# Two v projections called from the attention loop, and bias masks added in pairs, in a two-block transformer kernel

## The chip, the cores and the metric

The kernel runs on one core of a Trainium2 chip, as one program. The metric is the device time of that program in microseconds, the median over several runs. The core's engines work side by side, each through its own queue of instructions in order: TensorE (PE) multiplies matrices into PSUM, VectorE (DVE), ScalarE (ACT) and GpSimd (POOL) do the element-wise work, SyncE (SP) issues the loads.

## The reference

256 tokens of width 1024 go through two blocks. The first (MoBA attention, gated delta rule, a hierarchical mixture of experts) is not touched. The second block is this, cut to what matters:

```python
h = _modulate(_rms_norm(x, norm1_g), shift, scale)
q_a, k_a, v_a, q_b, k_b, v_b = _in_proj(h, w_in)            # latents
_, k_ac, v_ac, _, k_bc, v_bc = _in_proj(h_ctx, w_in)        # context
# heads a: rms norm of q and k per head, axial rope, window attention, sink
# heads b: rms norm of q and k per head, neighbourhood attention with bias rpb
o = concat([rms_norm(o_a) , rms_norm(o_b)]) * on            # per type, over its 512 columns
x = x + gate1 * (o @ w_out)
h = _modulate(_rms_norm(x, norm2_g), shift2, scale2)
x = x + gate2 * ((silu(h @ w_gate) * (h @ w_up)) @ w_down)
```

Both kinds of heads attend to 256 latent tokens and 256 context tokens, with 8 heads of 64 columns each.

## The kernel before, in words

**Products.** A product in block 2 is exact to nearly fp32: each operand is split into a high and a low part in fp32r, and `mm3` (L196) issues three matmuls, high by high, high by low, low by high (they are booked at L99). `split_w` (L168) splits a block of 256 weight rows or columns: ACT copies the high part in two pieces (L185), DVE or POOL subtracts for the low part in four (L192).

**Projections.** `proj_lat` (L1518) projects the latents on 256 columns of w_in: 48 matmuls into one PSUM bank of tag "big". The list `jobs` sets their order: k and v of heads a, k of heads b, then by `LORD = "bav"` q of heads b, q of heads a (`qa`, two halves), v of heads b (columns 1792 and 2048, tile `lvbp`, two halves). What is done with each product (`use`) comes one job later (`LAG`): for q `qk_heads` (head norm, rope at L1120 to L1123, transposes `pqk`, high and low halves at L1167 and L1171), for v a copy by DVE (L1539). With each projection the weights of the next are split, pieces 1 and 3 of the low part on POOL.

**Bias.** The bias of heads b comes by DMA into `bias0` and `bias1` (four heads each). `bias_mask` (L1571) adds a column mask to one head's bias on POOL; `BMU` says behind which unit.

**Attention.** The attention is cut in 16 units: type (a, then b), pair of heads m, half of the queries qt. `scores` (L1579) multiplies q by k into two "big" banks, adds the window mask or the bias by another matmul, takes the maximum on DVE (L1597), the exponential on ACT (L1607), and scales by the reciprocal sum, one head on ACT (L1616), the other on DVE (L1618). `turn` (L1623) transposes the probabilities through the two "tr" banks (`ptp`), one copy out by ACT, one by DVE (L1629). `outputs` multiplies by v into a bank `po` that two units share. `finish` (L1645) squares `po` on ACT (L1647), sums the squares over the columns with matmuls by a column of ones (`psq`, bank "sm"), copies the sum to `ssab` on DVE (L1651), and writes the scaled output as high and low part to `moh` and `mol` (L1652, L1653). The loop over the units computes the scores one unit ahead, and calls `hooks(i)` behind unit i.

**After.** `out_part` multiplies `moh`, `mol` by the four row blocks of w_out (wq0 to wq3; `pqa`, `pqb` in "big"), then the feed-forward part follows in 11 blocks (fg, fu, fd).

**What sets the order.** The framework's scheduler orders each engine's instructions when the program is built; the source order, the buffers and the few `after` calls bound it. PSUM in this stage: four "big" banks, two "tr", one "sm", one "mo". In SBUF a ring of nine 1 MB slots (`NRING`) holds the raw weight blocks, qa, qb, kAb0 and the biases; a slot is given again when its readers are done.

Of the kernel before, what the change touches and what calls it, by code (L numbers as in the profile page):

```python
# [10 lines left out]
F32R = mybir.dt.float32r  # L11
BF16 = mybir.dt.bfloat16
AF = mybir.ActivationFunctionType
ALU = mybir.AluOpType
# [3 lines left out]
P = 128  # L18
# [87 lines left out]
def tile_kernel(ctx: ExitStack, tc: tile.TileContext, I, out, dbg=None):  # L106
    nc = tc.nc
    PE, ACT, DVE, POOL, SP = Ordered(tc, nc.tensor), nc.scalar, nc.vector, nc.gpsimd, nc.sync
# [5 lines left out]
    S_ = {}  # L114
# [14 lines left out]
    def at(shape, tag, name, bufs=1, dt=F32):  # L129
        return S_["act"].tile(shape, dt, tag=tag, name=name, bufs=bufs)  # L130

    def open_part(name, psum):

        st = ExitStack()
        S_["tmp"] = st.enter_context(tc.tile_pool(name="tmp_" + name, bufs=1, reuse_waits="tile"))
        S_["ps"] = st.enter_context(tc.tile_pool(name="ps_" + name, bufs=1, space=PSUM, reuse_waits="tile"))
        S_["banks"] = psum
        return st
# [4 lines left out]
    def tmp_(shape, tag, name, bufs=1, dt=F32):  # L143
        return S_["tmp"].tile(shape, dt, tag=tag, name=name, bufs=bufs)

    def pt_(shape, tag, name):
        return S_["ps"].tile(shape, F32, tag=tag, name=name, bufs=S_["banks"][tag])

    def psm(shape, name, tag="sm"):
        return pso.tile(shape, F32, tag=tag, name=name)  # L150
# [174 lines left out]
    hth = at([P, 8, 256], "hth", "hth", dt=F32R)  # L325
    htl = at([P, 8, 256], "htl", "htl", dt=F32R)
# [393 lines left out]
    for tt in range(2):  # L720
        p = pt_([P, 4, P], "rec", "po")
# [149 lines left out]
    part = open_part("c1", {"gu": 2, "y": 2})  # L871
# [7 lines left out]
    for tt in range(2):  # L879
        ts = slice(tt * P, (tt + 1) * P)  # L880
        for i in range(2):
            p = pt_([P, 4, P], ("gu", "y")[tt], "pt")
# [6 lines left out]
    for tt in range(2):  # L889
        jk = tmp_([P, D], "jk", "jk", bufs=2, dt=BF16)  # L890
        if tt == 0:
            i = jk_ins = ACT.activation(jk, x[:, 0], AF.Square, accum_out=ssq[:, 0:1])
        else:
            i = DVE.scalar_tensor_tensor(jk, x[:, 1], 1.0, x[:, 1], op0=ALU.mult, op1=ALU.mult, accum_out=ssq[:, 1:2])
        if JKA[tt]:
            after(i, copies[2 + tt])
    v = tmp_([P, 2], "rv", "r1v")
# [149 lines left out]
    kvw = {}  # L1047
# [9 lines left out]
    part = open_part("c2", {"gu": 1, "y": 2, "tr": 1})  # L1057
# [45 lines left out]
    def head_norm(p, nh, dst, name):  # L1103

        src = p.rearrange("p t (n d) -> p t n d", d=64)
        sq = tmp_([P, 2, nh, 64], "hsq", "hsq", bufs=2)
        S_["hsq"] = ACT.activation(sq, src, AF.Square)
        ss = tmp_([P, 2, nh], "hss", "hss", bufs=4)
        DVE.tensor_reduce(ss, sq, axis=AX.X, op=ALU.add)
        r = rstd_of(ss.rearrange("p a b -> p (a b)"), 2 * nh, 1.0 / 64, EPS, name).rearrange("p (a b) -> p a b", a=2)  # L1110
        DVE.tensor_tensor(dst, src, bc(r, 64), op=ALU.mult)

    def do_rope(src, nh, i, dst):

        t2 = tmp_([P, 2, nh, 64], "hsq", "rt2", bufs=2)
        cosg, sing = rgt[:, i, :, 0], rgt[:, i, :, 1]
        for h in range(2):
            for b in range(2):
                o, i_ = 32 * h + 16 * b, 32 * h + 16 * (1 - b)
                DVE.tensor_tensor(t2[:, :, :, o:o + 16], src[:, :, :, i_:i_ + 16],  # L1120
                                  sing[:, :, None, o:o + 16].to_broadcast([P, 2, nh, 16]), op=ALU.mult)
        DVE.tensor_tensor(dst, src, cosg[:, :, None, :].to_broadcast([P, 2, nh, 64]), op=ALU.mult)
        DVE.tensor_tensor(dst, dst, t2, op=ALU.add)  # L1123

    def kv_a(p, s, tag):

        DVE.tensor_copy(va[s], p[:, :, P:256])
        kn_ = tmp_([P, 2, 2, 64], "qn_", "kn_", bufs=2)
        head_norm(p[:, :, 0:P], 2, kn_, "rka")
        if s == 0:  # L1130
            kr = tmp_([P, 2, 2, 64], "qn_", "kr", bufs=2)
            do_rope(kn_, 2, 1, kr)
            kn_ = kr
        kd = tmp_([P, 2, 2, 2, 64], "hsq", "kd", bufs=2)
        for tt in range(2):
            DVE.tensor_copy(kd[:, tt], kn_[:, tt][:, :, None, :].to_broadcast([P, 2, 2, 64]))
        pt = pt_([P, 2, 256], tag, "pka")
        for kvh in range(2):
            for tt in range(2):
                PE.transpose(pt[:, kvh, tt * P:(tt + 1) * P], kd[:, tt, kvh].rearrange("p a b -> p (a b)"), ident)  # L1140
        if s == 0:
            ACT.activation(kAa[s], pt, AF.Copy)
            DVE.tensor_tensor(kLa[s], pt, kAa[s], op=ALU.subtract)
        else:
            ACT.activation(kAa[s], pt, AF.Copy, scale=gcol[:, 1:2])
            DVE.scalar_tensor_tensor(kLa[s], pt, gcol[:, 1:2], kAa[s], op0=ALU.mult, op1=ALU.subtract)
# [32 lines left out]
    kAa, kLa, kAb, kLb, va, vb = ([None] * 2 for _ in range(6))  # L1179
# [96 lines left out]
    for u in range(8):  # L1276
        if u == IFU:
# [6 lines left out]
            part = open_part("ov", {"gu": 2, "y": 2})  # L1284
            overflow()
            part.close()
            part = open_part("c3", {"gu": 1, "y": 1, "tr": 1, "cx": 1})
# [28 lines left out]
        for i, (w, nm) in enumerate(((wg_, "eg"), (wu_, "eu"), (wd_, "ed"))):  # L1316
            if len(first[u]) == i:
                first[u].append([wexp(w, u, q, nm) for q in range(4)])
            if u >= IFU and i < 2 and CTX[u][i]:
                c0 = CTX[u][i][0]  # L1320
# [37 lines left out]
        p = pt_([P, 256], "tr", "pst")  # L1358
# [98 lines left out]
    for c0 in [c for part in LORD for c in {"v": (1792,), "a": (0, 256), "b": (768, 1024)}[part]]:  # L1457
        kvw[c0] = load_block(cols(w_in2, c0), "lat")
    hth, htl = mod_T(xf, [ss[:, 4, i:i + 1] for i in range(2)], mod[:, 1], mod[:, 0], "l",
                     lambda: kv_tiles(0, lambda shape, nm, dt: vb0 if nm == "vb0" else at(shape, nm, nm, dt=dt)))  # L1460
# [51 lines left out]
    qa = ring_tile("qa").rearrange("p (i m c) -> p i m c", i=2, m=4)  # L1512

    latw = {512: lka_w, 1280: lkb_w}
    seq = [1280, 1536] + [c for part in LORD for c in {"v": (1792, 2048), "a": (0, 256), "b": (768, 1024)}[part]]
    NEXT = dict(zip(seq, seq[1:]))

    def proj_lat(c0, name):  # L1518
        hi, lo = latw[c0]
        if c0 in NEXT:  # L1520
            n = NEXT[c0]
            latw[n] = split_w(kvw[n], "lat", pool=PLAT)
        p = pt_([P, 2, 256], "big", name + "p")
        for tt in range(2):
            ts = slice(tt * P, (tt + 1) * P)
            for k in range(8):
                mm3(p[:, tt], hth[:, k, ts], htl[:, k, ts], hi[:, k], lo[:, k], k == 0, k == 7)
        return p
# [3 lines left out]
    def uses(part):  # L1532

        for half in range(2):
            if part == "k":
                yield 1280 + 256 * half, "lkb", lambda p, half=half: qk_heads(p, half, 3, "tr", s=0)
            elif part == "v":
                vs = vb[0][:, :, half * 256:half * 256 + 256]
                yield 1792 + 256 * half, "lvb", lambda p, vs=vs: DVE.tensor_copy(vs, p)  # L1539
            elif part == "a":  # L1540
                yield 256 * half, "lq", lambda p, half=half: qk_heads(p, half, 0, "tr", q=qa)
            else:
                yield 768 + 256 * half, "lq", lambda p, half=half: qk_heads(p, half, 2, "tr", q=qb)

    ready = at([P, 1], "ready", "ready")
    jobs = [(512, "lka", lambda p: kv_a(p, 0, "tr"))] + [j for part in "k" + LORD for j in uses(part)]
    lag = []
    for n, (c0, name, use) in enumerate(jobs):
        if n == 3:
            after(ACT.activation(ready, mhalf[:, :1], AF.Exp), S_["hi"])  # L1550
        p = proj_lat(c0, name)
# [5 lines left out]
    bias = []  # L1557
# [9 lines left out]

    cm = cst3[:, C_CM:C_CM + 64]

    def bias_mask(h):  # L1570
        return POOL.tensor_tensor(bias[h], bias[h], cm[:, None, :].to_broadcast([P, 6, 64]), op=ALU.add)  # L1571


    moh = at([P, 8, 256], "hth", "moh", dt=F32R)
    mol = at([P, 8, 256], "htl", "mol", dt=F32R)
    rab = []
    ssab = at([P, 2, 2, 4], "ssab", "ssab")

# [65 lines left out]
    def finish(typ, m, po_):  # L1644
        k = 4 * typ + m  # L1645
        osq = at([P, 256], "mt", "osq2", bufs=3)
        ACT.activation(osq, po_, AF.Square)  # L1647
        psq = psm([P, 2], "psq")
        for tt in range(2):
            PE.matmul(psq[:, tt:tt + 1], lhsT=osq[:, tt * P:(tt + 1) * P], rhs=ones1, start=True, stop=True)  # L1650
        DVE.tensor_copy(ssab[:, typ, :, m], psq)  # L1651
        ACT.activation(moh[:, k], po_, AF.Copy, scale=onT[:, k:k + 1])  # L1652
        DVE.scalar_tensor_tensor(mol[:, k], po_, onT[:, k:k + 1], moh[:, k], op0=ALU.mult, op1=ALU.subtract)  # L1653
        if m == 3:
            ssum = at([P, 2], "ssum", "ssum", bufs=2)
            DVE.tensor_reduce(ssum, ssab[:, typ], axis=AX.X, op=ALU.add)
            rab.append(rstd_of(ssum, 2, 1.0 / 512, EPS, f"rab{typ}"))
# [11 lines left out]
    def hooks(i):  # L1669

        nonlocal g1B
        if i in G1U:
            g1B = row_bc(mod[:, 2, :, 0], kvc.tile([P, D], F32, tag="fB", name="g1B"))
        for h in BMU.get(i, ()):
            bias_mask(h)
        if i in WQU:
            w_blk2[WQU.index(i)] = w_block(WQU.index(i))
            after(S_["hi0"], S_["exp"])
# [59 lines left out]
    hth, htl = mod_T(x, norm_rows(x, "rf"), mod[:, 4], mod[:, 3], "f")  # L1738
# [70 lines left out]
PLAT = (1, 3)  # L1809
# [22 lines left out]
LORD = "bav"  # L1832
AORD = False
LATE = True
G1U = (5,)
BMU = {4: (0, 1), 5: (2, 3, 4, 5, 6, 7)}
WQU = (8, 10)
MORD = True
FOUT = [4, 2, 2, 2]
# [38 lines left out]
```

## Time and profile before

| what | us |
|---|---|
| runs, median (lowest, highest) | 837.55 (834.93, 837.75) |
| the profiled execution's own time | 832.61 |
| its span, first to last instruction | 830.8 |
| mean granted TensorE clock in it | 0.972 |
| PE busy (x instructions) | 752.4 (x6276) |
| DVE busy | 425.1 (x933) |
| ACT busy | 301.7 (x533) |
| POOL busy | 108.1 (x94) |

Times in the trace count from the start of the span. The projections of v run from 509.6 to 522 us, the attention units from 525.7 to about 617, the out-projection ends at about 620, the feed-forward part fills the rest. A bracket behind a row of the timeline tells how long the engine was idle before it, and who ended that.

### The profile page before, as it was taken

Reading aid. Unit: us, or ns where it says so; the run is one execution under the profiler, and the core shown is the slowest. Engines: PE = TensorE matmul, PEld = TensorE weight load, DVE = VectorE, ACT = ScalarE, POOL = GpSimd, SP = SyncE. Lnnn points to the kernel's source line nnn. Section 1 sums busy time; section 2 is a strip of 40 time slices with the busy share of each in tenths; the row PEclk is TensorE's granted clock in tenths of the full one; section 3 lists DMA queues with packets and bytes.
Section 4 is the critical chain, followed back from the end, with each engine's and each line's share of the span. In section 5 each row is a group of like instructions: output and inputs, shape, how many; then the busy total and the mean of one; then the engine's idle time right before and its main releaser. Section 6 shows DMA issues by size and latency. Waiting matters only on the chain.

```text
span 830.8 us, 15017 instructions
## 1 busy us (share of the span) xinstructions
PE 752.4 (91%) x6276; PEld 604.0 (73%) x6276; DVE 425.1 (51%) x933; ACT 301.7 (36%) x533; POOL 108.1 (13%) x94
## 2 busy tenths in 40 slices
PE   7999999999799976787778999699987999999997
PEld 7887887966644424374544889688866999999996
DVE  5767543465712212203222789988655654545545
ACT  5532233443420010001114663488515343443441
POOL 5011000053000000000000476400122100000000
PEclk9999999999799998999999999999998999999999
DMA  7999778577589999999989416011441754555201
GB/s 214 356 386 388 283 284 302 203 278 330 206 337 420 420 418 418 391 409 409 410 354 326 130 20 181 30 51 52 153 152 67 238 203 161 194 192 167 98 2 50
DMA packets 87590, 201.21 MB, mean 242 GB/s; under 512 B 15496, under 2 KB 63040, under 8 KB 75232
## 3 DMA queue, kind: packets, MB, share of 16 engines
q1 hardware_dynamic: 87328, 200.12, 65.0%
q8 instruction: 50, 0.82, 0.4%
q0 software_dynamic: 192, 0.11, 0.1%
q14 instruction: 20, 0.16, 0.1%
HBM read 199.27 MB, written 1.05 MB: 241 GB/s over the span
## 4 chain that ended last, share of the span: by engine, by line
PE 39%; DMA 7%; DVE 7%; issue 4%; POOL 2%; ACT 2%; SPq 1%; DVEq 0%; POOLq 0%; ACTq 0%
PE pfu L99 8%; PE pfg L99 7%; PE pf L99 7%; PE sc L99 3%; DMA ed<-in_w_down_dram 3%; DMA kv<-in_w_in_dram 2%; PE po L99 2%; PE ptp L102 2%; PE pgu L99 2%; PE pqa L99 1%; PE pqb L99 1%; DMA eg<-in_w_gate_dram 1%; POOL rq L218 1%; PE ckbp L99 1%; SPq L164 1%
## 5 line engine op out<-in xcount | busy, mean ns | idle before, releaser
L99 PE MATMUL pfu<-hif,fuh 128*128 128x256 f32 x176 | 50.5, 287 | 1.6 <-ACT fuh L185 1.6
L99 PE MATMUL pfu<-hif,ful 128*128 128x256 f32 x176 | 50.5, 287 | 0.8 <-POOL ful L192 0.8
L99 PE MATMUL pfu<-lof,fuh 128*128 128x256 f32 x176 | 50.4, 286 | 0.0
L99 PE MATMUL pfg<-lof,fgh 128*128 128x256 f32 x160 | 45.4, 284 | 0.0
L99 PE MATMUL pfg<-hif,fgh 128*128 128x256 f32 x160 | 45.4, 284 | 0.0
L99 PE MATMUL pfg<-hif,fgl 128*128 128x256 f32 x160 | 45.3, 283 | 0.0
L99 PE MATMUL pyd<-ed,hid 128*32 128x512 f32 x256 | 39.8, 642 | 4.6 <-ACT hid L1378 2.4
L192 DVE TENSOR_TENSOR fdl<-fd,fdh 128x512 fp32r<-128x512 f32 x44 | 27.5, 688 | 28.9 <-ACT fdh L185 28.9
L1363 ACT ACTIVATE sg<-pgu,r1s 128x256 f32<-128x256 f32 x8 | 3.8, 473 | 94.4 <-PE pgu L99 94.4
L99 PE MATMUL pgu<-eg,xg 128*32 128x256 f32 x512 | 34.9, 397 | 2.9 <-DMA eg<-in_w_gate_dram 1.8
L99 PE MATMUL pgu<-eu,xg 128*32 128x256 f32 x512 | 34.1, 391 | 2.5 <-DMA eu<-in_w_up_dram 2.5
L99 PEld LDWEIGHTS pfu<-hif,fuh 128*128 128x128 f32 x176 | 34.4, 195 | 1.8 <-ACT fuh L185 1.8
L185 ACT ACTIVATE fdh<-fd 128x1024 fp32r<-128x1024 f32 x22 | 22.1, 1052 | 36.9 <-issue 36.9
L185 ACT ACTIVATE fuh<-fu 128x1024 fp32r<-128x1024 f32 x22 | 22.1, 1052 | 36.5 <-issue 28.6
L99 PE MATMUL pf<-fdl,fh 128*128 128x512 f32 x88 | 35.1, 399 | 0.0
L99 PEld LDWEIGHTS pfu<-hif,ful 128*128 128x128 f32 x176 | 34.3, 195 | 1.0 <-POOL ful L192 1.0
L99 PE MATMUL pf<-fdh,fh 128*128 128x512 f32 x88 | 34.7, 395 | 0.0
L99 PEld LDWEIGHTS pfu<-lof,fuh 128*128 128x128 f32 x176 | 34.4, 195 | 0.0
L99 PE MATMUL pf<-fdh,fl 128*128 128x512 f32 x88 | 34.0, 392 | 0.0
L1389 DVE TENSOR_TENSOR yl<-pyd,yh 128x512 fp32r<-128x512 f32 x16 | 11.1, 691 | 42.9 <-ACT yh L1388 35.0
L192 DVE TENSOR_TENSOR fgl<-fg,fgh 128x512 fp32r<-128x512 f32 x40 | 27.7, 754 | 9.3 <-ACT fgh L185 9.3
L99 PEld LDWEIGHTS pfg<-hif,fgh 128*128 128x128 f32 x160 | 30.8, 193 | 0.4
(713 smaller groups left out, 2158.2 us busy)
## 6 DMA issues: line engine op xcount, KB each, us to landing
eg<-in_w_gate_dram SPq DMA_DIRECT2D x32, 1024.0 KB, 17.5
eu<-in_w_up_dram SPq DMA_DIRECT2D x32, 1024.0 KB, 17.8
ed<-in_w_down_dram SPq DMA_DIRECT2D x32, 1024.0 KB, 15.2
wmod<-in_w_mod_dram SPq DMA_DIRECT2D x24, 1024.0 KB, 10.6
fg<-in_w_gate_dram SPq DMA_DIRECT2D x11, 1024.0 KB, 5.4
fu<-in_w_up_dram SPq DMA_DIRECT2D x11, 1024.0 KB, 5.4
fd<-in_w_down_dram SPq DMA_DIRECT2D x11, 1024.0 KB, 5.0
kv<-in_w_in_dram SPq DMA_DIRECT2D x5, 1024.0 KB, 15.3
```

Source lines behind the costliest of these rows:

```text
L99: return self._keep(self.engine.matmul(*args, **kwargs))
L102: return self._keep(self.engine.transpose(*args, **kwargs))
L164: SP.dma_start(v, src)
L185: S_["hi"] = ACT.activation(hf[:, s], vf[:, s], AF.Copy)
L192: i = (POOL if c in pool else DVE).tensor_tensor(lf[:, s], vf[:, s], hf[:, s], op=ALU.subtract)
L218: S_["pow"] = POOL.tensor_tensor(r, v, mhalf[:, :n], op=ALU.pow)
L1363: ACT.activation(sg, pgu[:, 0], AF.Silu, scale=r1s[:, u:u + 1])
L1389: DVE.tensor_tensor(yl, py, yh, op=ALU.subtract)
```

## The change

The v projections leave `jobs`. They are called from the unit loop, behind unit 0 and unit 2 (`VU`), each into the one bank "sm"; the split of column block 1792 is made when it is called. `psq` goes from "sm" to the two "tr" banks. The masks are added in four pairs, behind units 3, 5, 7 and 9; each pair reads a copy of the column mask (`cmc`) that ACT makes after the exponential last issued. `moh` and `mol` no longer take the buffers of `hth` and `htl` (which the v projections still read), but two slots of the ring, so that every later tile of the ring moves to another slot.

```diff
-    seq = [1280, 1536] + [c for part in LORD for c in {"v": (1792, 2048), "a": (0, 256), "b": (768, 1024)}[part]]
+    seq = [1280, 1536] + [c for part in LORD[:2] for c in {"a": (0, 256), "b": (768, 1024)}[part]]
...
-    def proj_lat(c0, name):
+    def proj_lat(c0, name, p=None):
+        if c0 not in latw:
+            latw[c0] = split_w(kvw[c0], "lat", pool=PLAT)
...
-        p = pt_([P, 2, 256], "big", name + "p")
+        p = p or pt_([P, 2, 256], "big", name + "p")
...
-            elif part == "v":
-                vs = vb[0][:, :, half * 256:half * 256 + 256]
-                yield 1792 + 256 * half, "lvb", lambda p, vs=vs: DVE.tensor_copy(vs, p)
...
-    jobs = [(512, "lka", lambda p: kv_a(p, 0, "tr"))] + [j for part in "k" + LORD for j in uses(part)]
+    jobs = [(512, "lka", lambda p: kv_a(p, 0, "tr"))] + [j for part in "k" + LORD[:2] for j in uses(part)]
...
-    def bias_mask(h):
-        return POOL.tensor_tensor(bias[h], bias[h], cm[:, None, :].to_broadcast([P, 6, 64]), op=ALU.add)
-
-
-    moh = at([P, 8, 256], "hth", "moh", dt=F32R)
-    mol = at([P, 8, 256], "htl", "mol", dt=F32R)
+    def bias_masks(hs):
+
+        c = at([P, 64], "cmc", "cmc", bufs=2)
+        after(ACT.copy(c, cm), S_["exp"])
+        for h in hs:
+            POOL.tensor_tensor(bias[h], bias[h], c[:, None, :].to_broadcast([P, 6, 64]), op=ALU.add)
+
+
+    moh = ring_tile("moh").rearrange("p (k c) -> p k c", k=8)
+    mol = ring_tile("mol").rearrange("p (k c) -> p k c", k=8)
...
-        psq = psm([P, 2], "psq")
+        psq = pt_([P, 2], "tr", "psq")
...
-        for h in BMU.get(i, ()):
-            bias_mask(h)
+        if i in BMU:
+            bias_masks(BMU[i])
+        if i in VU:
+            half = VU.index(i)
+            vs = vb[0][:, :, half * 256:half * 256 + 256]
+            DVE.tensor_copy(vs, proj_lat(1792 + 256 * half, "lvb", psm([P, 2, 256], "lvbp")))
...
-BMU = {4: (0, 1), 5: (2, 3, 4, 5, 6, 7)}
+BMU = {3: (0, 1), 5: (2, 3), 7: (4, 5), 9: (6, 7)}
+VU = (0, 2)
```

The order of the instructions moves at three places. The first is PE's queue where the attention units begin (`lvbp` is v's projection, `sc` a bank of scores, `pqk` the transposes of a half of qa). Before, all 96 matmuls of v stand ahead of unit 0's scores:

```order
L99 MATMUL lvbp<-lath,lol 128x256
L99 MATMUL sc_5171<-k_3520,qa 128x256 x2
L99 MATMUL sc_5171<-k_4360,qa 128x256 x2
L99 LDWEIGHTS identb
L99 MATMUL sc_5171<-maskc,identb 128x128
L99 MATMUL sc_5172<-k_3520,qa 128x256 x2
```

Now the scores of units 0 and 1 come with 19 of the 96 still to do:

```order
L99 MATMUL sc_5082<-k_4360,qa 128x256 x2
L99 LDWEIGHTS identb
L99 MATMUL sc_5081<-maskn,identb 128x128
L99 LDWEIGHTS identb
L99 MATMUL sc_5082<-maskn,identb 128x128
L99 MATMUL lvbp<-lath,lol 128x256
L99 MATMUL lvbp<-lath,hil 128x256
L99 MATMUL lvbp<-latl,hil 128x256
```

17 matmuls of v stand behind unit 1's scores, then the four transposes `pqk` of qa's half 1, then two more of v, then unit 2's scores; 48 stand ahead of the transposes of half 0, and 29 between them and unit 0's scores.

The second place is DVE's queue in the same stretch. Before, with L1171 (the low halves of qa) of half 0 behind the rope of half 1:

```order
L216 TENSOR_SCALAR rqv<-hss 128x8
L1539 COPY mixed<-lvbp 128x2x256
L1111 TENSOR_TENSOR qn__5071<-lqp,rq 128x512
L1120 TENSOR_TENSOR rt_5082<-qn__5071,mixed 128x8x16 x4
L1122 TENSOR_TENSOR qr__5081<-qn__5071,mixed 128x512
L1171 TENSOR_TENSOR qa<-pqk,qa 64x512 x2
L1123 TENSOR_TENSOR qr__5081<-qr__5081,rt_5082 128x512
```

Now:

```order
L192 TENSOR_TENSOR latl<-kv_4320,lath 128x512 x2
L216 TENSOR_SCALAR rqv<-hss 128x8
L1682 COPY mixed<-lvbp 128x2x256
L1171 TENSOR_TENSOR qa<-pqk,qa 64x512 x2
L1111 TENSOR_TENSOR qn__5006<-lqp,rq 128x512
L1120 TENSOR_TENSOR rt_5017<-qn__5006,mixed 128x8x16 x4
L1122 TENSOR_TENSOR qr__5016<-qn__5006,mixed 128x512
L1600 TENSOR_REDUCE st<-sc_5055 128x1
```

L1171 of half 0 has moved ahead of the norm and the rope of half 1, and L1171 of half 1 now comes 23 rows further on, behind the first scalings.

The third place is PE's queue at the end of a pair of units (`ptp` are transposes in a "tr" bank, `psq` the sums of squares). Before, for the second pair:

```order
L102 MATMUL ptp<-cst,prb_5424 128x128 x4
L99 MATMUL sc_5641<-kAb_3523,qb 128x256
L99 MATMUL sc_5641<-kLb_3524,qb 128x256
L99 MATMUL sc_5641<-kAb_4478,qb 128x256
L99 MATMUL sc_5641<-kLb_4438,qb 128x256
L99 MATMUL sc_5641<-bias_5149,mixed 128x256
L99 MATMUL psq<-ones_96,osq_5398 128x1 x2
L102 MATMUL ptp<-cst,prb_5426 128x128 x4
```

Now, for the same pair:

```order
L99 MATMUL sc_5583<-kLb_4438,qb 128x256
L99 MATMUL sc_5583<-bias_5033,mixed 128x256
L99 MATMUL psq<-ones_96,osq_5402 128x1 x2
L102 MATMUL ptp<-cst,prb_5368 128x128 x4
L102 MATMUL ptp<-cst,prb_5370 128x128 x4
L99 MATMUL po<-pT_5441,va_4361 64x128
L102 MATMUL ptp<-cst,prb_5428 128x128 x4
L99 MATMUL sc_5645<-kAb_3523,qb 128x256
```

psq shares the two banks with the groups of transposes that stand directly behind it. Five of the eight pairs read so, with two groups of transposes behind psq.

## Rows read from the trace of the kernel before

**Rows 1.** The page: PE's busy time and share, and the chain that ended last.
```profile
PE 752.4 (91%) x6276; PEld 604.0 (73%) x6276; DVE 425.1 (51%) x933; ACT 301.7 (36%) x533; POOL 108.1 (13%) x94
...
PE 39%; DMA 7%; DVE 7%; issue 4%; POOL 2%; ACT 2%; SPq 1%; DVEq 0%; POOLq 0%; ACTq 0%
```

**Rows 2.** Windows of PE: stretch, length, busy us (instructions), granted clock, DMA share, GB/s.
```profile
522.00:526.00 4.00, 0.45 (x3) 0.93 0.00 0
526.00:530.00 4.00, 4.00 (x24) 0.65 0.00 0
...
538.00:555.00 17.00, 16.68 (x160) 1.00 0.18 64
555.00:586.00 31.00, 30.60 (x273) 1.00 0.11 36
586.00:620.00 34.00, 33.53 (x220) 1.00 0.53 174
```

**Rows 3.** Timeline of PE, first scores: start, us, engine, line, operation.
```profile
525.73 1.22 PE L99 MATMUL sc<-k,qa 128*128 128x256 f32 x4 [3.55 <-DVE qa L1171]
...
527.94 1.13 PE L99 MATMUL sc<-k,qa 128*128 128x256 f32 x4
...
531.79 0.74 PE L99 MATMUL sc<-k,qa 128*128 128x256 f32 x4 [1.66 <-ACT prb L1607]
...
535.94 0.74 PE L99 MATMUL sc<-k,qa 128*128 128x256 f32 x4 [0.96 <-ACT prb L1607]
```

**Rows 4.** Timeline of DVE: the rope of qa's two halves, and L1171.
```profile
513.61 0.99 DVE L1120 TENSOR_TENSOR rt<-qn__4987,mixed 128x128 f32<-128x128 f32 x4
514.53 0.68 DVE L1122 TENSOR_TENSOR qr__4997<-qn__4987,mixed 128x512 f32<-128x512 f32 x1
...
520.16 3.41 DVE L1120 TENSOR_TENSOR rt<-qn__5071,mixed 128x128 f32<-128x128 f32 x4
523.49 1.48 DVE L1122 TENSOR_TENSOR qr__5081<-qn__5071,mixed 128x512 f32<-128x512 f32 x1
525.00 1.41 DVE L1171 TENSOR_TENSOR qa<-pqk,qa 64x512 fp32r<-64x512 f32 x2
```

**Rows 5.** Timeline of POOL: the masks.
```profile
519.37 8.82 POOL L1571 TENSOR_TENSOR bias<-bias,mixed 128x384 f32<-128x384 f32 x8
```

**Rows 6.** The tile lvbp: ns min/median/max, first and last start, forms.
```profile
L99 PE MATMUL lvbp<-lath,hil x32: 278/283/284, 509.6 to 521.7; 128*128 128x256 f32 x32
...
L1539 DVE COPY mixed<-lvbp x2: 692/692/693, 517.7 to 527.4; 128x512 f32<-128x512 f32 x2
```

**Rows 7.** Timeline of ACT: a small activation.
```profile
533.25 0.19 ACT L1601 ACTIVATE st<-st 128x2 f32<-128x2 f32 x1
```

**Rows 8.** Windows of all engines: PE, PEld, DVE, ACT, POOL busy, clock, DMA.
```profile
540.00:550.00 10.00, 10.00 (x99) 8.81 (x96) 9.24 (x26) 9.71 (x26) 0.00 (x0) 1.00 0.07 18
```

**Rows 9.** Groups of DVE by line, 539 to 620: busy us, mean ns, idle before.
```profile
L1618 DVE TENSOR_SCALAR prb<-prb,st 128x512 f32<-128x512 f32 x14 | 6.7, 481 | 0.1
...
L192 DVE TENSOR_TENSOR wq3l<-wq,wq3h 128x512 fp32r<-128x512 f32 x4 | 3.8, 1007 | 0.3 <-ACT wq3h L185 0.3
...
L192 DVE TENSOR_TENSOR wq1l<-wq,wq1h 128x512 fp32r<-128x512 f32 x4 | 2.6, 685 | 0.0
```

**Rows 10.** Timeline: eight transposes, and the end of the last pair of units.
```profile
536.58 1.06 PE L102 MATMUL ptp<-cst,prb 128*128 128x128 f32 x8
...
616.11 0.70 PE L99 MATMUL po<-pT,vb 128*64 128x128 f32 x7
616.85 0.38 ACT L1647 ACTIVATE osq<-po 128x256 f32<-128x256 f32 x1 [8.80 <-PE po L99]
...
617.28 0.61 PE L99 MATMUL psq<-ones,osq 128*128 128x1 f32 x4 [0.47 <-ACT osq L1647]
...
618.03 0.15 DVE L1651 COPY ssab<-psq 128x2 f32<-128x2 f32 x1
```

**Rows 11.** The page: DMA issues, KB each, us from issue to landing.
```profile
fg<-in_w_gate_dram SPq DMA_DIRECT2D x11, 1024.0 KB, 5.4
```

## The prediction

> **What bounds the kernel now.** I read the page first: PE is busy for 91% of the span, and PE is 39% of the chain that ended last [rows 1]. So the question for any change is whether PE has idle time at the place, and who ends it. The table of windows around the change answers the first half [rows 2]. From 538 to 555 PE is busy 16.68 of 17 us, from 555 to 586 30.60 of 31, from 586 to 620 33.53 of 34: the attention units leave nothing to win, and what is added to PE there, as work or as a wait, is paid in full. In front of that lies a hole: from 522 to 526 PE is busy 0.45 us of 4, and from 526 to 530 it is busy throughout, but at a granted clock of 0.65, a mean between the two levels (1.2 and 2.4 GHz) right after the idle time.
>
> The timeline of PE fills the hole in [rows 3]. The first scores start at 525.73 after 3.55 us of waiting for DVE's subtraction at L1171, which makes the low halves of qa. Three groups of four score matmuls there take 1.22, some 1.2 and 1.13 us; the same group at 531.79 takes 0.74. Then come waits of 1.66 and 0.96 us for the first exponentials. Together 3.55 + (3.5 - 2.2) + 1.66 + 0.96 = 7.5 us: that is the ceiling of what the start can give back.
>
> The reason for the late L1171 is on DVE [rows 4]. The rope's four multiplies took 0.99 us for qa's half 0 and 3.41 us for half 1, L1122 0.68 and then 1.48; the second set ran while POOL added the eight bias masks, 8.82 us in a row from 519.37 [rows 5]. That is 2.42 + 0.80 = 3.2 us lost by DVE on the very chain that PE waits for.
>
> **The change, part by part.**
>
> *The v projections.* 96 matmuls stay 96, so PE's work is the same; each starts 0.13 us after the one before, waits included, 0.12 without (32 of each of the three kinds, the first kind from 509.6 to 521.7, so 12.1 us for 31 triples; 0.28 us each by their pipelined ends) [rows 6]. By the listed order 48 still run first, then the transposes of qa's half 0, then 29 more, then the scores of units 0 and 1, then the last 19 around the transposes of half 1. Only 19, or 2.3 us, really lie behind the first scores. By hand, from the rows' durations: the first 48 end at 515.4; half 0's rope, by the durations in [rows 4], is ready at about 518, so PE now idles 2.5 us there where it used to have the second half's v to do. The 29 need the bank "sm", freed by the copy of v's first half (0.69 us [rows 6]), which stands on DVE behind two low splits: about 520.2, another 1.7 us of idling. They end at 523.7. The scores then run to 526.3, without a wait for half 1's rope, since L1171 of half 0 is ahead of it on DVE, and the 19 with the transposes to 528.9. The first exponential, at 530.96 before, can start near 527.5; four exponentials later unit 4's scores, at 535.94 in [rows 3], come at about 533.4. **Lead: 2.5 us.** Bounds: 5 (two thirds of the ceiling) if the hand schedule's idling is shorter and the clock stays high, 1 if the rope or the copy is a microsecond later than I think.
>
> *The masks.* The eight adds leave the rope (that is in the lead) and go in pairs of some 2 x 1.05 us, from 8.82 / 8 with a little contention [rows 5], behind the exponentials of units 4, 6, 8 and 10. Unit 8's scores are the first that need a mask, three units later, so no PE wait. The four small ACT copies cost about 0.2 us each by the nearest small activation [rows 7], 0.8 us in all on an engine that is busy 9.71 of 10 us from 540 to 550; DVE is busy 9.24 there and PE 10.00 [rows 8]. The adds now run beside DVE's scalings (0.48 us each [rows 9]) in that full stretch. The trace shows what POOL does to a DVE operation with both inputs in SBUF: wq3l, split while POOL adds, takes 1007 ns, wq1l without POOL 685 [rows 9], and the rope went from 0.99 to 3.41 us [rows 4], while the subtraction at L1171, which reads PSUM, took 0.70 each right beside the masks. I take 0.5 us for copies and masks: between 0, if DVE's slack swallows them, and 3.4, if both pairs in the full stretch (4.2 us) hold DVE and only its 0.8 us of slack is there.
> The Trainium skill (SBUF — State Buffer, "Who interferes with whom") says that DVE and GpSimd share one port pair as an exclusive lock: a DVE instruction with two SBUF inputs, or in a two-port mode, and a GpSimd one that reads SBUF block one another for a whole instruction. The trace agrees, with the 3.41 against 0.99 us above; by the rule alone, all 8.4 us of masks would stand against DVE's scalings and small operations, and it would be the rival "masks" below at its full price.
>
> *psq moves into the transposes' banks.* [Rows 10] show one pair's end: the last po matmul ends at 616.81, the square runs on ACT to 617.23, psq starts at 617.28, the copy to ssab ends at 618.18. That is 1.36 us in which a bank belongs to this sum. Before it had a bank of its own, "sm". Now it takes one of the two that the transposes turn over, and by the order five of the eight pairs have two groups of transposes right behind psq, of which the second needs psq's bank. Four transposes are 0.53 us (half of 1.06 for eight [rows 10]), psq's own issue 0.46, so with an idle DVE nothing is lost: 617.28 + 0.99 is later than 618.18. But DVE is 92% busy [rows 8], and its next operation may be a 0.69 us reduce; and the first group now has only the other bank, whose evacuation copy is not done either. I take 0.5 us for each of five: 2.5. A sixth pair (units 12 and 13) issues psq directly behind its po, where twelve matmuls stood between before: the wait for the square is the 0.47 us in [rows 10]. **Sum 3.0 us**; bounds 0 and 6 x 1.36 = 8.2.
>
> *The tail.* The transposes and outputs of units 14 and 15 come at the very end without out-projection matmuls between them; each then waits for a 0.69 us copy less what is between. Two such copies, 0.3 and 0.7 us less the overlap: 0.7 (0 to 1.5). The last exponential stands behind four big ACT splits, but some 70 matmuls precede its transposes.
>
> *The ring slots.* wq2, wq3 and fg load later, into slots that come free after units 11 and 7 and after the first out-projection splits. A block of this size lands 5.4 us after its issue [rows 11], and the last slot to come free for one of these three, wq1's after its split, is free some 8 us before fg's split, which the listed order puts behind unit 15's scores. What hides the loads is the attention units; I cost them at 0, and at up to 2 us if that cover is gone.
>
> Sum: -2.5 + 3.0 + 0.7 + 0.5 = **+1.7 us**. The profiled execution took 832.6 us, so 834.3 for its like; it lies 4.9 us under the median of the runs shown, 837.55, so I forecast **839.2 us**. A measurement of this kernel tells about 0.5% (4.2 us) from no change.
>
> **The rivals.**
> - *The start pays, the banks don't cost* (0.25). DVE's copies of psq are early, the clock holds, the lead is 5: 837.55 - 5 = 832.5. For it: 3.2 us of contention and the low clock do go [rows 2, 4]. Against: 77 of the 96 are still in front of the scores.
> - *The bank is waited for in full* (0.12), slower: the place is psq's bank in "tr", the price 1.36 us in each of six pairs, from the point where DVE's queue is never empty when psq ends. 8.2 - 2.5 + 0.7 + 0.5 = +6.9: 844.4. For it: no slack on PE after 538 and DVE at 9.24 of 10 [rows 2, 8].
> - *The change does not do what it says* (0.08): the scores start no earlier because the 29 wait for the one bank. Without the lead +4.2: 841.7, on the border of what can be told.
> - *Masks* (0.08): both pairs in the full stretch hold DVE; +1.7 - 0.5 + 3.4 = +4.6: 842.1.
>
> **How the numbers follow.** The forecast has 0.47, with its own range from 835.5 to 842.5. Faster by over 0.5% is nearly all of the first rival and a little of the forecast's edge: 0.26. Slower is the second, most of the fourth, half of the third and the edge: 0.24. That leaves 0.50. The range runs from 832.0, under the first rival, to 844.5, at the second; beyond lie combinations such as a lead of 5 with nothing lost, or 1 with all banks waited for.
>
> **What would show it.** Right: the first exponential near 527.5 and unit 4's scores near 533.4; rope at 1 us in both halves; new rows "ptp waits for DVE ssab" or for a copy of pT, some 0.5 us each, five times from 538 on, and psq waiting for osq twice instead of once; the last out-projection ending about 2 us later than now. Wrong: if PE is as full after 538 as now and the end moves forward by the lead, the bank term was empty; if scalings at L1618 stretch beyond 1 us and ptp waits for them, it was the masks; if PE idles over 5 us between 515 and 526, the lead never came.

## The result, and the profile after

| | before | changed |
|---|---|---|
| runs, median (lowest to highest), us | 837.38 (833.95 to 838.84) | 845.94 (845.01 to 848.98) |
| profiled execution, its span | 832.61, 830.8 | 845.61, 843.8 |

(Before has three more runs here than the 837.55 shown with the prediction.)

The ratio is 1.0118, with a 95% interval from 1.0088 to 1.0147: **slower by 1.2%**, where no measurable change was forecast, and above the top of the range (844.5). The page of the changed kernel answers to [rows 1] with PE's busy time and the chain:

```profile
PE 762.5 (90%) x6276; PEld 610.5 (72%) x6276; DVE 423.4 (50%) x933; ACT 303.4 (36%) x537; POOL 107.8 (13%) x94
...
PE 61%; DMA 17%; DVE 9%; issue 5%; ACT 3%; POOL 2%; SPq 2%; DVEq 0%; POOLq 0%; ACTq 0%
```

PE has the same 6276 matmuls and is busy 10.1 us longer. The first projection of block 2's latents starts at 461.00 in the trace of before and at 462.87 in this one, so 1.9 us of the difference between the two traces lie ahead of the change. I therefore compare two stretches, read from PE's timelines: **start**, from the last q matmul to the first transposes of probabilities, and **units**, from there to the last matmul of the out-projection, always from the start of one matmul to the start of the other. Before they are 27.1 and 83.8 us, in the changed kernel 28.6 and 93.3.

The start, in PE's timeline of the changed kernel (it answers to [rows 3]):

```profile
520.98 0.67 PE L102 MATMUL pqk<-cst,qr__4989 128*128 128x128 f32 x4 [3.63 <-DVE qr__4989 L1123]
522.99 0.55 PE L99 MATMUL lvbp<-lath,hil 128*128 128x256 f32 x1 [1.33 <-ACT qa L1167]
523.34 0.41 PE L99 MATMUL lvbp<-latl,hil 128*128 128x256 f32 x1
...
528.85 0.63 PE L99 MATMUL sc<-k,qa 128*128 128x256 f32 x4
...
538.81 1.20 PE L99 MATMUL sc<-k,qa 128*128 128x256 f32 x4 [2.15 <-DVE qa L1171]
...
539.93 1.92 PE L102 MATMUL ptp<-cst,prb 128*128 128x128 f32 x8
```

The hole has not closed, it has moved forward. PE waits 3.63 us for the rope of half 0 and 1.33 us more before the other 29 matmuls of v. The first exponential comes at 532.83, where before has it at 530.96: less the 1.9 us ahead of the change, that is no lead at all. Unit 4's scores, at 538.81, wait 2.15 us for L1171 of half 1, and the eight transposes behind them take 1.92 us where [rows 10] have 1.06. Windows of PE show the granted clock there (columns as in [rows 2]):

```profile
520.00:523.00 3.00, 0.68 (x5) 0.74 0.00 0
523.00:528.00 5.00, 5.00 (x23) 0.50 0.60 210
528.00:534.00 6.00, 6.00 (x53) 0.98 0.00 0
534.00:538.00 4.00, 2.62 (x21) 1.00 0.01 2
538.00:541.00 3.00, 2.19 (x11) 0.58 0.00 0
```

From 523 to 528 PE is at the lower of its two levels, right after idling, and v's matmuls start 0.21 us apart there instead of 0.12; only the last five of the 29 are back at 0.12. DVE and POOL show why half 0 is late (DVE's rows answer to [rows 4], the last one is half 1's rope; of POOL's two rows the first stands beside half 0's rope, the second is a pair of masks among the units):

```profile
514.40 2.96 DVE L1120 TENSOR_TENSOR rt<-qn__4979,mixed 128x128 f32<-128x128 f32 x4
517.29 0.68 DVE L1122 TENSOR_TENSOR qr__4989<-qn__4979,mixed 128x512 f32<-128x512 f32 x1
518.00 1.51 DVE L1173 SCALAR_TENSOR_TENSOR qb<-pqk,gcol,qb 64x512 fp32r<-64x512 f32 x2
...
520.15 0.68 DVE L1123 TENSOR_TENSOR qr__4989<-qr__4989,rt 128x512 f32<-128x512 f32 x1
...
525.08 0.90 DVE L1120 TENSOR_TENSOR rt<-qn__5006,mixed 128x128 f32<-128x128 f32 x4
```

```profile
514.21 2.61 POOL L192 TENSOR_TENSOR latl<-kv,lath 128x512 fp32r<-128x512 f32 x2 [0.83 <-ACT lath L185]
...
555.69 2.65 POOL L1574 TENSOR_TENSOR bias<-bias,cmc 128x384 f32<-128x384 f32 x2 [7.34 <-ACT cmc L1572]
```

Half 1's rope is free of the masks (0.90 us), as forecast. But half 0's takes 2.96 us, beside POOL's low splits of the v weights, which now come 2.9 us later in the trace than in before. All six kernels with v moved show this (2.87 to 2.97 us), and with v in its old place every trace has 0.98 to 1.00. Two more DVE operations of heads b and a reduction stand in front of its last step.

The units, by PE's waits from 505 to 650 (us in total, times, longest). Of before, between 545 and 620, the view has only the 0.5 us for the square and 0.4 us for g1B, a broadcast made by ACT:

```profile
PE ptp L102 <- ACT pT L1632: 1.5, 2, 0.8
PE psq L99 <- ACT osq L1650: 1.4, 3, 0.5
...
PE po L99 <- DVE pT L1632: 0.5, 1, 0.5
...
PE ptp L102 <- DVE ssab L1654: 0.3, 1, 0.3
PE po L99 <- ACT pT L1632: 0.2, 1, 0.2
```

And one end of a pair, in the changed kernel's timeline of all engines:

```profile
558.09 0.50 PE L99 MATMUL psq<-ones,osq 128*128 128x1 f32 x4
558.45 0.63 PE L102 MATMUL ptp<-cst,prb 128*128 128x128 f32 x4
558.48 0.48 DVE L1656 SCALAR_TENSOR_TENSOR mol<-po,onT,moh 128x256 fp32r<-128x256 f32 x1
558.89 0.68 DVE L1600 TENSOR_REDUCE st<-sc 128x1 f32<-128x512 f32 x1
559.48 0.47 DVE L1621 TENSOR_SCALAR prb<-prb,st 128x512 f32<-128x512 f32 x1
559.88 0.15 DVE L1654 COPY ssab<-psq 128x2 f32<-128x2 f32 x1
559.90 0.66 PE L102 MATMUL ptp<-cst,prb 128*128 128x128 f32 x4 [0.82 <-ACT pT L1632]
```

psq has ended at 558.59. Its copy to ssab, of 0.15 us, starts 1.29 us later, behind three other operations in DVE's queue, and all that time the sum holds one of the two banks that the transposes need; the other bank waits for ACT's copy.

### The profile page after: what moved, and what is told of

Same layout as the page of the kernel before. It is cut to its first block, busy times and chain, and to the rows that moved or that the text cites. A ratio compares the mean times of both kernels' runs of the same rounds, so it can differ in the third digit from the quotient of the medians.

```text
span 843.8 us, 15027 instructions
## 1 busy us (share of the span) xinstructions
PE 762.5 (90%) x6276; PEld 610.5 (72%) x6276; DVE 423.4 (50%) x933; ACT 303.4 (36%) x537; POOL 107.8 (13%) x94
## 4 chain that ended last, share of the span: by engine, by line
PE 61%; DMA 17%; DVE 9%; issue 5%; ACT 3%; POOL 2%; SPq 2%; DVEq 0%; POOLq 0%; ACTq 0%
PE pfu L99 8%; PE pfg L99 7%; PE pf L99 7%; DMA ed<-in_w_down_dram 6%; PE po L99 5%; DMA eg<-in_w_gate_dram 5%; PE sc L99 3%; PE pmod L99 3%; PE pgu L99 3%; DMA eu<-in_w_up_dram 2%; PE ptp L102 2%; PE pu L99 2%; DMA kv<-in_w_in_dram 2%; PE pyd L99 2%; PE pqa L99 1%
## 5 line engine op out<-in xcount | busy, mean ns | idle before, releaser
L99 PE MATMUL pgu<-eu,xg 128*32 128x256 f32 x512 | 37.0, 419 | 2.5 <-DMA eu<-in_w_up_dram 2.5
L185 ACT ACTIVATE fuh<-fu 128x1024 fp32r<-128x1024 f32 x22 | 22.1, 1053 | 36.5 <-issue 28.6
L192 DVE TENSOR_TENSOR fgl<-fg,fgh 128x512 fp32r<-128x512 f32 x40 | 27.7, 754 | 9.4 <-ACT fgh L185 9.4
L99 PEld LDWEIGHTS pgu<-eu,xg 128*32 128x32 f32 x512 | 18.7, 120 | 18.6 <-issue 6.3
```

Of the source, the lines that this page charges most:

```text
L99: return self._keep(self.engine.matmul(*args, **kwargs))
L185: S_["hi"] = ACT.activation(hf[:, s], vf[:, s], AF.Copy)
L192: i = (POOL if c in pool else DVE).tensor_tensor(lf[:, s], vf[:, s], hf[:, s], op=ALU.subtract)
```

## The experiments

Theory "bank": psq in the transposes' banks costs. Theory "start": moving v leaves PE idle and slow. Theory "masks": the masks beside the units hold DVE. All runs are in one table; "faster" or "slower" is against before. The runs were made in several rounds, in which before had medians from 836.5 to 837.4; each ratio is against before of its own round.

| run | median, us | ratio (95% interval) | start | units |
|---|---|---|---|---|
| before | 837.4 | | 27.1 | 83.8 |
| b_again (before, second trace) | 835.1 (one) | | 28.4 | 84.7 |
| changed | 845.9 | 1.0118 (1.0088, 1.0147) | 28.6 | 93.3 |
| b_psq_tr | 841.2 | 1.0074 (1.0040, 1.0107) | 27.3 | 91.3 |
| a_psq_sm | 837.7 | 1.0001 (0.9981, 1.0020) | 27.7 | 84.2 |
| a_masks_early | 845.3 | 1.0101 (1.0076, 1.0127) | 29.0 | 93.7 |
| b_masks_late | 831.4 | 0.9927 (0.9904, 0.9950) | 24.3 | 85.4 |
| b_masks_ring | 830.2 | 0.9926 (0.9897, 0.9955) | 23.8 | 84.1 |
| a_psq_sm_v02 | 839.5 | 1.0038 (1.0017, 1.0060) | 23.6 | 92.8 |
| b_masks_psq_tr | 842.2 | 1.0059 (1.0033, 1.0085) | 23.8 | 91.7 |
| b_masks_psq_tr_act | 838.3 | 1.0025 (1.0003, 1.0047) | 24.3 | 90.6 |
| b_masks_psq_tr_later | 835.2 | 0.9978 (0.9956, 1.0000) | 23.8 | 85.7 |
| a_psq_sm_v_big | 844.7 | 1.0104 (1.0078, 1.0131) | 26.6 | 95.8 |
| a_psq_sm_warm | 839.5 | 1.0045 (1.0023, 1.0066) | 26.9 | 88.3 |

**The parts one by one.** First psq alone, on the kernel before (b_psq_tr):

```diff
-        psq = psm([P, 2], "psq")
+        psq = pt_([P, 2], "tr", "psq")
```

> The kernel before with one line of the change: the sums of squares psq take one of the transposes' two banks. Theory 'bank' (the units lost 9.4 us between the first transposes and the last out-projection because psq shares these banks, and the order is bent around that): slower by 6 to 10 us, with ptp waits for copies of pT and for ssab as in the changed kernel, while the start (first scores to first transposes) stays as before. Theory 'start' (moving v leaves PE idle and at a low clock, and the units follow late): within 2 us of before. Theory 'masks': within 2 us of before.

The start is that of before, the units are 7.4 us longer. The median rises by 3.8 us only, below the 6 to 10 expected; in part that is because the first trace of before was an early one (against its second trace, below, start and units together are 5.4 us longer). Theory "bank" holds, with a smaller price in the median than expected.

Then the changed kernel with that line undone and v behind units 0 and 1 (a_psq_sm):

```diff
-        psq = pt_([P, 2], "tr", "psq")
+        psq = psm([P, 2], "psq")
...
-VU = (0, 2)
+VU = (0, 1)
```

> The changed kernel with psq back in its own bank sm, and the two v projections called behind units 0 and 1, so that both are done with sm before the first psq; the order of PE up to the first transposes is that of the changed kernel. Theory 'bank': most of the loss is gone, some 1 to 3 us slower than before, by the start alone. Theory 'start': still 7 to 10 us slower than before. Theory 'masks': still 5 us slower or more.

The time is equal to before's, and the units are back at 84.2 us. What is left of the change is worth nothing in sum, though the masks have moved.

The changed kernel with the masks' old place (a_masks_early), and before with the new one (b_masks_late):

```diff
-BMU = {3: (0, 1), 5: (2, 3), 7: (4, 5), 9: (6, 7)}
+BMU = {4: (0, 1), 5: (2, 3, 4, 5, 6, 7)}
```

> The changed kernel with the masks as before (behind units 4 and 5 in the source, all eight in a row on POOL, reading the constant itself); PE's order is word for word that of the changed kernel. Theory 'bank' and theory 'start': as slow as the changed kernel or up to 3 us slower still (the rope of half 1 again beside the masks). Theory 'masks' (the adds beside the units' scalings hold DVE): 4 us faster than the changed kernel or more.

> The kernel before with the masks alone moved, in pairs behind the exponentials of units 4, 6, 8 and 10 through the ACT copy. Theory 'bank' and theory 'start': the rope of half 1 takes 1 us again, the scores start 2 to 3 us earlier, and the time is 1 to 3 us under before's. Theory 'masks': 3 us slower than before or more.

Theory "masks" falls twice: putting them back gains the changed kernel nothing (845.3 against 845.9), and moving them alone makes the kernel before **faster by 0.7%**. The timeline of PE in b_masks_late shows the lead that the prediction hoped for, and what eats a part of it:

```profile
522.85 0.74 PE L99 MATMUL sc<-k,qa 128*128 128x256 f32 x4 [0.25 <-DVE qa L1171]
...
528.29 0.74 PE L99 MATMUL sc<-k,qa 128*128 128x256 f32 x4 [2.26 <-ACT prb L1611]
...
529.91 1.22 PE L99 MATMUL sc<-k,qa 128*128 128x256 f32 x4
...
532.98 1.22 PE L99 MATMUL sc<-k,qa 128*128 128x256 f32 x4 [0.63 <-ACT prb L1611]
```

The wait of 3.55 us in [rows 3] is 0.25, and the rope of half 1 took 0.90 us. Then the exponentials are waited for (2.26 us), and four score matmuls take 1.22 us behind that wait, at 529.91 and 532.98. The median fell by 6.0 us, more than the 1 to 3 expected. Start and units together are only 1.3 us shorter than in the first trace of before and 3.4 us shorter than in its second, so not all of the 6.0 us is located.

b_again asked where the first trace of before was early:

> The kernel before once more, for a second trace: its profiled execution was 4.8 us under the median of its runs, those of the variants lie within 1 us of theirs. If the missing time lies ahead of the change, the first projection of block 2's latents starts some 4 us later than the 461.0 of the first trace, and the stretch from there to the end is as long as before. If it lies in the attention units, the stretch from the first transposes to the last out-projection is longer than 83.8 us.

Of its 2.5 us over the first trace, 0.7 lie ahead of the change and 2.2 in the two stretches, with the feed-forward part giving 0.4 back. Its windows of PE from 526 on:

```profile
526.00:530.00 4.00, 3.56 (x18) 0.63 0.00 0
530.00:534.00 4.00, 2.34 (x17) 0.93 0.00 0
534.00:538.00 4.00, 3.37 (x15) 0.50 0.00 0
538.00:542.00 4.00, 3.80 (x24) 0.66 0.00 2
```

And those of the first trace of before, for the second and third of these stretches:

```profile
530.00:534.00 4.00, 2.21 (x17) 1.00 0.00 0
534.00:538.00 4.00, 3.04 (x26) 1.00 0.00 2
```

The same program had nearly the full clock back from 530 to 534 and lost it again, where the first trace kept it. The changed kernel's two stretches, 121.9 us, are 8.7 longer than b_again's 113.1, close to the difference of the medians (8.6); against the first trace they are 10.9 longer.

**v's place, alone.** b_masks_ring is b_masks_late with moh and mol in the ring's slots, so it differs from a_psq_sm by v's place only:

```diff
-    moh = at([P, 8, 256], "hth", "moh", dt=F32R)
-    mol = at([P, 8, 256], "htl", "mol", dt=F32R)
+    moh = ring_tile("moh").rearrange("p (k c) -> p k c", k=8)
+    mol = ring_tile("mol").rearrange("p (k c) -> p k c", k=8)
```

> The kernel before with the masks moved and with moh and mol in two slots of the ring, so that every later block of weights moves to another slot; v and psq as before. It differs from a_psq_sm by v's place alone. Theory 'v's place takes the lead away': within 1 us of b_masks_late (831.4), 6 us faster than a_psq_sm. Rival 'the ring's later loads cost': 835 to 838, and v's place costs next to nothing.

The ring's new slots cost nothing that can be told, and this kernel has the lowest median of the study (830.2). v's place costs 7.5 us by the medians, 6 by the ratios. Between the two traces 3.9 us lie in the stretch "start" (27.7 against 23.8), and 3.2 us lie ahead of the change. Why is open; the mean granted clock is 0.963 in the one execution and 0.970 in the other.

a_psq_sm_v02 keeps the change's `VU = (0, 2)` with psq in sm, which puts 48 matmuls of v behind the first units' scores; a_psq_sm_v_big puts all 96 there, in the score banks:

```diff
-            DVE.tensor_copy(vs, proj_lat(1792 + 256 * half, "lvb", psm([P, 2, 256], "lvbp")))
+            DVE.tensor_copy(vs, proj_lat(1792 + 256 * half, "lvb"))
```

> The changed kernel with psq in its own bank and v behind units 0 and 2 as in the change: the first psq now stands between the two v projections in bank sm, so that 48 of the 96 matmuls of v really come behind the first units' scores. Theory 'v's place takes the lead away, by PE's idle time before the first scores and the low clock after it': the idle time ahead of the scores stays (some 4 to 5 us), the scores come 5 us earlier than in a_psq_sm, and the 48 are paid between the units; 834 to 838, no faster than before. Rival 'v only has to come late enough': the lead is kept, 830 to 832.

> a_psq_sm with v's two projections in two of the four score banks instead of sm, so that all 96 matmuls come behind unit 0's and 1's scores, as fillers of the first units. Theory 'v in front of the scores covers PE's wait for the rope': PE idles some 8 us before the first scores, they start at 520 to 522 and run at the low clock; the 96 (11.5 us) fill what the exponentials leave open, but 832 to 838, no better than b_masks_ring (830.2). Rival 'fillers between the first units are worth more than in front of them': under 829.

For v02 the first theory holds, with a median above its band (839.5): its start is as short as without the move, but start and units together are 8.5 us longer than b_masks_ring's, for 48 matmuls of 0.12 us (5.8). In v_big PE stood still before the scores, start and units are 14.5 us longer for 96 such matmuls (11.5), and the time was worse than the 838 that the first theory gave as its worst:

```profile
522.20 1.09 PE L102 MATMUL pqk<-cst,qr__4989 128*128 128x128 f32 x4 [9.30 <-DVE qr__4989 L1123]
525.29 1.01 PE L99 MATMUL sc<-k,qa 128*128 128x256 f32 x3 [2.00 <-DVE qa L1171]
```

In before, v's matmuls ran there, and PE waited 3.55 us ahead of its first scores; that was their use in front of the scores.

Does the low clock behind the idle time set the price? a_psq_sm_warm puts 24 transposes, whose result nobody reads, on PE ahead of the rope:

```diff
             n2 = tmp_([P, 2, 4, 64], "qn_", "qr_", bufs=2)
+            if half == 0:
+                junk = pt_([P, 4, P], tag, "junk")
+                for r in range(24):
+                    PE.transpose(junk[:, r % 4], n_[:, r // 2 % 2, 2 * (r % 2):2 * (r % 2) + 2].rearrange("p a b -> p (a b)"), ident)
             do_rope(n_, 4, 0, n2)
```

> a_psq_sm with 24 transposes more, whose result nobody reads, put on PE between the norm of qa's half 0 and its rope (about 2.9 us of work that the change does not need). Theory 'the idle time before qa's transposes lets the clock fall, and the 29 matmuls of v behind them pay for it': the 29 start 0.12 us apart instead of 0.21, the scores start 1 to 3 us earlier than in a_psq_sm in spite of the added work, and the time is 1 to 4 us under a_psq_sm's 837.7. Rival 'the idle time itself is the price, the clock a side effect': the same time as a_psq_sm or slower.

```profile
512.57 2.81 PE L102 MATMUL junk<-cst,qn__4979 128*128 128x128 f32 x24
518.97 0.63 PE L102 MATMUL pqk<-cst,qr__4989 128*128 128x128 f32 x4 [2.17 <-DVE qr__4989 L1123]
523.65 0.74 PE L99 MATMUL sc<-k,qa 128*128 128x256 f32 x4 [2.74 <-DVE qa L1175]
...
527.21 0.41 PE L99 MATMUL lvbp<-latl,hil 128*128 128x256 f32 x1
```

The first scores came 2.8 us earlier, counted from the last q matmul, but v's next matmuls, from 527, again start 0.21 us apart, start and units together became 3.4 us longer (the added transposes take 2.8), and the time was no better than a_psq_sm's (839.5 against 837.7), as the rival had it. The experiment also moved the order of v and of the units (the second 48 matmuls of v now all stand behind the first scores), so it shows that filling the gap at that one place buys nothing here, not what the clock alone is worth.

**The bank, alone.** b_masks_psq_tr is b_masks_late with psq in "tr"; a second run lets ACT copy psq to ssab, a third issues the sums one step later in the source:

```diff
-        DVE.tensor_copy(ssab[:, typ, :, m], psq)
+        ACT.copy(ssab[:, typ, :, m], psq)
```

```diff
-        if late:
-            finish(*late.pop())
+        sums = finish(*late.pop()) if late else None
...
         outputs(*un, po_, pTs)
+        if sums:
+            sums()
```

(`finish` here returns its psq part as a function.)

> The kernel before with the masks moved and psq in the transposes' banks, v and ring as before. Theory 'the bank costs by itself, whatever the start': 7 to 9 us over b_masks_late (838.5 to 840.5), with the same waits of ptp and po as in b_psq_tr. Rival 'the bank costs only where the start is late': within 4 us of b_masks_late.

> b_masks_psq_tr with the copy from psq to ssab made by ACT instead of DVE. Theory 'the bank is held while the copy stands in DVE's queue': the two waits of ptp for ssab (1.2 us in b_masks_psq_tr) go, 1 to 3 us faster. Rival 'two banks for three users are too few, whoever copies': within 1 us of it, since ACT's queue is as full as DVE's and the pT copies wait behind the same work.

> b_masks_psq_tr with the sums of squares issued one step later in the source (behind the next unit's outputs instead of ahead of its scores); psq still takes a transposes' bank, and PE's order has one group of transposes behind psq and then scores, where b_masks_psq_tr has two groups. Theory 'the place of psq, ahead of two groups that need both banks, is what costs': the stretch from the first transposes to the last out-projection falls from 91.7 to 84 to 87 us, 831 to 836 in all. Rival 'two banks for three users cost wherever psq stands': 90 us or more, within 2 us of b_masks_psq_tr.

By itself the bank costs 6.3 us in the units (91.7 against b_masks_late's 85.4, which it differs from by this line alone), wherever the start lies; against b_masks_ring's 84.1 it would be 7.6. The medians, 842.2 against 831.4, show some 11, more than the 7 to 9 expected: the traced execution has the lowest time of its kernel's eight, at a mean granted clock of 0.970 where the others had 0.961 to 0.965. With ACT's copy the units shorten by 1.2 us, and one wait of ptp for ssab (0.8 us) is left, where there were two (1.2 us); the median falls by 3.9 us, but the two intervals overlap, so what the copy's engine matters stays open. Issued later, the units are back at 85.7 us. Rows of PE's waits, first of b_masks_psq_tr, then of b_masks_psq_tr_later:

```profile
PE ptp L102 <- DVE ssab L1655: 1.2, 2, 0.7
PE psq L99 <- ACT osq L1651: 0.9, 2, 0.5
...
PE ptp L102 <- ACT pT L1633: 0.7, 1, 0.7
PE po L99 <- DVE pT L1633: 0.5, 1, 0.5
```

```profile
PE ptp L102 <- DVE pT L1633: 0.5, 1, 0.5
PE psq L99 <- ACT osq L1651: 0.5, 1, 0.5
```

The sum still lives in a transposes' bank there; no row for ssab is left. In the traces, then, **6.1 of the 6.3 us go when psq is issued later**, no longer ahead of two groups of transposes that need both banks. By the medians it is 7.0 of some 11: 835.2 stays 3.8 us above b_masks_late, and the intervals of the two ratios don't meet. The traced execution again has the lowest time of its kernel's (831.92), so no trace shows where these 3.8 us lie, and that the bank costs nothing at a better place is not shown. The edit also moves the copy and the last sum on DVE with psq. The named waits of b_masks_psq_tr are some 3 us; the rest is in matmuls that start farther apart, which these runs don't divide further. On the changed kernel itself this edit was not tried.

## Why the prediction was wrong, step by step

- **"Lead: 2.5 us" failed, and with it the sign of the start.** The step was "half 0's rope, by the durations in [rows 4], is ready at about 518". It took its 0.99 us from a place without POOL beside it, while the change itself moves POOL's low splits into that place: the multiplies took 2.96 us, and the transposes came at 520.98, 1.1 us late when the 1.9 us ahead of the change are taken off. The idle time was 3.63 + 1.33 us instead of 2.5 + 1.7 (the copy that frees "sm" ended at 522.84, so the wait of the third rival is in the 1.33), and most of the 29 matmuls ran at the lower level, 0.21 us apart: they took 5.9 us where the sum had 3.5. Half 1's L1171, behind the first scalings in DVE's queue, then held unit 4's scores for 2.15 us, which the sum had nowhere. The start came out 1.5 us longer than in the first trace of before, and level with b_again.
- **The contention of masks and rope was right, but it was the masks' part alone.** 3.2 us were forecast to leave DVE; b_masks_late won 2.8 us in the start and 6 us in the median. v's move took it all back (a_psq_sm: 1.0001). The prediction put two effects of opposite sign into one "lead".
- **"Sum 3.0 us" for psq was the mis-sized term.** It priced waits of PE and left the spacing of PE's matmuls as it was. The place was right, DVE's queue was not empty when psq ended, and the waits on the rows come to about that sum: 1.5 for pT, 0.3 for ssab, 0.9 more for osq, 0.7 at po, together 3.4 (though not as five waits of 0.5 us). But the units grew by 9.0 us over a_psq_sm's. PE's windows of the units, first a_psq_sm, then the changed kernel (columns as in [rows 2]):

```profile
540.51:624.73 84.22, 83.34 (x660) 1.00 0.30 100
539.93:633.19 93.26, 89.01 (x661) 0.99 0.27 90
```

  PE's idle time grew by 3.4 us, its busy time by 5.7 with the same matmuls, and the sum had nothing for the second. 0.9 of the 5.7 us is the lower clock at the first eight transposes (1.92 us against a_psq_sm's 1.04). The rest is matmuls that start farther apart at or near the full clock; as their ends are modelled, short waits may hide in it, and its cause stays open. The rival "the bank is waited for in full" had the right side and was given 0.12; its 8.2 us (1.36 us six times) came near the measured 6.3 to 9.0 by luck, since no wait of PE on the rows is that long.
- **"I take 0.5 us for copies and masks" holds.** b_masks_ring's units are within 0.5 us of before's. (b_masks_late's are 1.6 longer; its first eight transposes ran at the lower clock.) The masks do hold DVE in the changed kernel: wq0l takes 887 ns in the mean where the split of wq1l, without POOL, has 685 [rows 9]. That agrees with the Trainium skill (SBUF — State Buffer, "Who interferes with whom"), by which a DVE instruction with two SBUF inputs and a GpSimd one that reads SBUF hold each other up. The scalings have 537 against 481 ns, nearly all of it by a single one, of 1.27 us beside a pair of masks. But DVE's time there is not PE's: with the masks out of the units, a_masks_early's units are no shorter (93.7).

```profile
L1621 DVE TENSOR_SCALAR prb<-prb,st 128x512 f32<-128x512 f32 x14 | 7.5, 537 | 0.2
L192 DVE TENSOR_TENSOR wq0l<-wq,wq0h 128x512 fp32r<-128x512 f32 x4 | 3.4, 887 | 0.0
```

- **The tail (0.7) and the ring (0)** came out right: the tail has one wait of po for pT, of 0.49 us, and PE's waits behind 505 us name no load.
- **The baseline** was read right as early (4.9 us under the median), but not where: part of it was the clock in the very stretch of the change, where the same program differs by 2.2 us from one execution to the next.

## What to carry to other kernels

When a change moves several things, cost each with the others absent: here one part gained 0.7%, one gave that back, one lost 1%. Before a piece of work is moved away from a stretch with a wait, ask what it was covering: here v's matmuls in front of the scores ran while PE had to wait anyway, and behind them they cost their full time or more. And a small result that is lent a bank of a busy pair should be issued where the users of that pair have other work to do next, which here gave back most of the price; look at what follows it in the engine's order, not at its 0.15 us. Price a changed order by the length of the whole stretch, too: here the named waits were a third to a half of what it cost.

## What the runs showed of the hardware that was not expected

The granted clock differs between executions of one program at the same place: 0.50 from 534 to 538 in b_again's trace, where the first trace of before had the scores at full speed (0.74 us for four at 535.94, [rows 3], against 1.23 at 537.45 in b_again). Putting work into one gap moved the slow matmuls to the next place (from those of v at 524 in a_psq_sm to those at 527 in a_psq_sm_warm) and did not remove them.
